# Moving the buffers that TensorE reads to whole kilobytes of a partition, in a two-layer decoder trunk

## The chip, the core and the metric

The kernel runs on one core of a Trainium2 chip. The metric is the device time of one execution in microseconds (us). It is given as the median of several runs. A separate execution is profiled, and its trace is what the views below come from. The engines are PE (TensorE, matmuls), PEld (TensorE's loads of stationary operands), DVE (VectorE), ACT (ScalarE), POOL (GpSimd) and SP (SyncE, which here issues the transfers).

## What is computed

The reference is a decoder of two layers on 256 tokens of width 2048, all in float32:

```python
h = x
for i in range(2):
    a = rmsnorm(h, attn_norm[i])
    h = h + (sb_dilated_mixer(a, ...) if i % 2 == 0 else fox_mixer(a, ...))   # q/k/v projection, 16 heads, output projection
    h = h + conv_ffn(rmsnorm(h, ffn_norm[i]), w_up[i], conv_w[i], conv_b[i], w_down[i])   # 2048 -> 2 x 5632 -> 2048
    gate = sigmoid(rmsnorm(h, ple_norm[i]) @ w_ple_gate[i])                    # 2048 -> 2048
    h = h + gate * (p[i] @ w_ple[i])                                           # 256 -> 2048
return rmsnorm(h, final_norm)
```

Layer 0's mixer has eight stick-breaking heads and eight heads of a dilated window. Layer 1's has 16 heads with forget gates. Nearly all of the arithmetic lies in the products with weights: `w_in` (2048 x 6144), `w_out`, `w_up` (2048 x 11264), `w_down` (5632 x 2048) and `w_ple_gate`.

## The kernel before

**Layout.** Activations lie with features on the 128 partitions and the 256 tokens along the free dimension. `h` holds 16 such slices. A product needs more precision than one pass of the one-pass type float32r gives, so both operands are split into a high and a low part (both float32r). `act0` and `act1` (line 114) hold an activation as `[128, 16, 2, 256]`: for each slice k of 128 features the 256 high parts and then the 256 low parts, which is 2 KB of a partition for each k. `pact` holds the same for the per-layer embedding.

**Weights.** They stream in once, in an order that the host prepares (`UNITS`, `GROUPS`). `issue_group` (line 144) loads up to 8 KB a partition into one of three `wr` buffers. `split_unit` (line 158) makes a unit's high part by a copy on ACT (line 165) and its low part by a subtraction on DVE (line 166), in one of four `w` buffers of 8 KB, as `[128, k, 2, 256]`. Up to three units stand ready ahead of TensorE (`LOOK`, line 170).

**Products.** `gemm_unit` (line 194) is the core. A unit has usually four slices k and 256 output features, taken as two halves j of 128. For each half TensorE runs, for the k of the unit, a matmul with the high weights as stationary operand and the 512 columns of `act[:, k]` (high and low) as moving stream (line 208), and then, for the same k, a matmul with the low weights and the 256 high columns `act[:, k, 0, :]` (line 211). So a half is a group of four streams of 512 columns and four of 256; in the down projection some units have three k. `gemm_v` (line 236) does the same for the value projection with the operands exchanged: the `w` buffer is streamed (lines 243 and 246) and 128 columns of `act` are loaded as weights. Where `flat` is set (line 199), and in the last product of all (line 736), there are three streams of 256 columns instead: high with high, high with low, low with high. `ple_up` (line 367) uses this with `pact`. `gemm_vf` (line 250) streams 272 columns of a `w` buffer.

**Around the products.** Each product goes to one of two PSUM buffers (`mm`). ACT copies one part out into a work tile `jn` or `jh`, DVE adds the other (lines 263 to 274). Work tiles of 2 KB come from the tag `t2` (line 134), which has seven buffers: `jn`, `jh`, `sq`, the two results `yg` and `yv` of a convolution group, `nd` and others. A buffer is given out again when its last reader is done. The attention is put among the units by a counter (`defer`, `tick`).

**Placement.** Pools get their place in the order in which they are opened, and tiles in a pool in the order in which they are made. Four small constants come first, so that the first pool, `cpool`, begins at byte 16,512 of a partition, 128 past a whole KB. By the addresses in the compiled kernel `h` lies there, `act0` at 32,896, `act1` at 65,664 and `pact` at 98,432 (all 128 past a whole KB), the three `wr` buffers at 138,432 and on and the four `w` buffers at 163,008, 171,200, 179,392 and 187,584 (all 192 past a whole KB). [...] Of the tiles that TensorE streams, one lies at a whole KB, the small `c2` of the forget gates (64 partitions, lines 491 and 493).

Of the kernel before, what the change touches and what calls it, by code (L numbers as in the profile page):

```python
# [10 lines left out]
F32 = mybir.dt.float32  # L11
F32R = mybir.dt.float32r
# [5 lines left out]
P = 128  # L18
D = 2048
S = 256  # L20
# [5 lines left out]
KT = D // P  # L26
# [78 lines left out]
def trunk(ctx: ExitStack, tc: tile.TileContext, xT, pT, pos, gains, conv, bf, cst, wst, out):  # L105
    nc = tc.nc

    cpool = ctx.enter_context(tc.tile_pool(name="cpool", bufs=1))
    wpool = ctx.enter_context(tc.tile_pool(name="wpool", bufs=1))
    work = ctx.enter_context(tc.tile_pool(name="work", bufs=1))  # L110
    psum = ctx.enter_context(tc.tile_pool(name="psum", bufs=1, space=bass.MemoryType.PSUM))

    h = cpool.tile([P, KT, S], F32, name="h")
    bufs = [cpool.tile([P, KT, 2, S], F32R, name=f"act{i}") for i in range(2)]
    pact = cpool.tile([P, 2, 2, S], F32R, name="pact")
    pl = cpool.tile([P, KT, S], F32, name="pl")
    gn = cpool.tile([P, 7, KT], F32, name="gn")
    cv = cpool.tile([P, DEPTH, 2 * FT, 4], F32, name="cv")
# [13 lines left out]
        return psum.tile([P, 2, 512], F32, name=name, tag="at", bufs=2)  # L132

    def t2_tile(name, shape=(P, 2, S), dt=F32):
        return work.tile(list(shape), dt, name=name, tag="t2", bufs=7)

    def t3_tile(name, shape=(P, 768), dt=F32):
        return work.tile(list(shape), dt, name=name, tag="t3", bufs=4)
# [124 lines left out]
    def joined(ps):  # L263
        t = t2_tile("jn")
        nc.scalar.copy(out=t, in_=ps[:, :, 1, :])  # L265
        nc.vector.tensor_add(out=t, in0=t, in1=ps[:, :, 0, :])  # L266
        return t

    def add_to_h(op, ps):
        hs = h[:, 2 * op:2 * op + 2, :]  # L270
        t = t2_tile("jh")
        nc.scalar.copy(out=t, in_=ps[:, :, 1, :])
        nc.vector.tensor_add(out=hs, in0=hs, in1=ps[:, :, 0, :])
        nc.vector.tensor_add(out=hs, in0=hs, in1=t)
# [17 lines left out]
    def norm_squares(op):  # L292
        hs = h[:, 2 * op:2 * op + 2, :]
        if op == 0:
            nc.scalar.activation(out=acc, in_=hs, func=AF.Square)
        else:
            sq = t2_tile("sq")
            nc.scalar.activation(out=sq, in_=hs, func=AF.Square)
            nc.vector.tensor_add(out=acc, in0=acc, in1=sq)
# [538 lines left out]
```

## Time and profile before

| | |
|---|---|
| median of 3 runs | 2476.81 us (2476.19 to 2476.83) |
| the profiled execution | 2476.15 us |
| its span, first to last instruction | 2474.4 us |
| granted TensorE clock, mean | 0.997 |
| busy: PE, PEld, DVE, ACT | 2453.4, 2145.1, 1715.1, 1320.2 us |
| moved by DMA | 457.20 MB, mean 185 GB/s |

A busy PE is not a PE at its peak: the profile gives the start of each matmul, and models its end, so a matmul's duration overlaps with the next one's. What a matmul costs in a row of them is the distance from its start to the start of the next. The timeline merges neighbours of one line into a row, "x4" for four, and the start of the following row closes the stretch.

### The profile page before, as it was taken

Reading aid. Unit: us, or ns where it says so; the run is one execution under the profiler, and the core shown is the slowest. Engines: PE = TensorE matmul, PEld = TensorE weight load, DVE = VectorE, ACT = ScalarE, POOL = GpSimd, SP = SyncE. Lnnn points to the kernel's source line nnn. Section 1 sums busy time; section 2 is a strip of 40 time slices with the busy share of each in tenths; the row PEclk is TensorE's granted clock in tenths of the full one; section 3 lists DMA queues with packets and bytes.
Section 4 is the critical chain, followed back from the end, with each engine's and each line's share of the span. In section 5 each row is a group of like instructions: output and inputs, shape, how many; then the busy total and the mean of one; then the engine's idle time right before and its main releaser. Section 6 shows DMA issues by size and latency. Waiting matters only on the chain. (4 is left out here: it accounts for less than half of the span.)

```text
span 2474.4 us, 34810 instructions
## 1 busy us (share of the span) xinstructions
PE 2453.4 (99%) x14270; PEld 2145.1 (87%) x14270; DVE 1715.1 (69%) x2386; ACT 1320.2 (53%) x1747; POOL 2.5 (0%) x8
## 2 busy tenths in 40 slices
PE   8999999999999999999999999999999999999997
PEld 7888888888888888888888888888888888888887
DVE  7767667776577657777765555677765776677776
ACT  6554455555455545556554444555544554455564
POOL 0000000000000000000000000000000000000000
PEclk9999999999999999999999999999999999999998
DMA  7444455555555555555454444555555555555553
GB/s 264 170 171 170 170 188 187 190 188 198 188 190 187 183 195 187 199 177 204 175 176 166 167 162 165 188 192 188 194 188 187 189 188 190 195 192 183 185 194 119
DMA packets 66431, 457.20 MB, mean 185 GB/s; under 512 B 7408, under 2 KB 7424, under 8 KB 16608
## 3 DMA queue, kind: packets, MB, share of 16 engines
q1 hardware_dynamic: 66096, 454.53, 51.9%
q8 instruction: 111, 1.82, 0.3%
q0 software_dynamic: 176, 0.46, 0.1%
q14 instruction: 48, 0.39, 0.0%
HBM read 452.86 MB, written 2.10 MB: 184 GB/s over the span
## 5 line engine op out<-in xcount | busy, mean ns | idle before, releaser
L166 DVE TENSOR_TENSOR w<-wr,w 128x1024 fp32r<-128x1024 f32 (+2 forms) x882 | 1049.2, 1191 | 500.0 <-ACT w L165 497.8
L165 ACT CAST w<-wr 128x1024 fp32r<-128x1024 f32 (+2 forms) x882 | 904.6, 1026 | 676.7 <-PE psd L211 179.2
L208 PE MATMUL psu<-act,w 128*128 128x512 f32 x2816 | 767.9, 394 | 0.0
L208 PEld LDWEIGHTS psu<-act,w 128*128 128x128 f32 x2816 | 476.7, 188 | 59.9
L211 PEld LDWEIGHTS psu<-act,w 128*128 128x128 f32 x2816 | 428.2, 188 | 63.8
L211 PE MATMUL psu<-act,w 128*128 128x256 f32 x2816 | 437.3, 277 | 0.0
L208 PE MATMUL psd<-act,w 128*128 128x512 f32 x1408 | 388.8, 394 | 0.0
L208 PEld LDWEIGHTS psd<-act,w 128*128 128x128 f32 x1408 | 236.4, 188 | 26.7
L211 PEld LDWEIGHTS psd<-act,w 128*128 128x128 f32 x1408 | 219.1, 188 | 34.7
L211 PE MATMUL psd<-act,w 128*128 128x256 f32 x1408 | 224.6, 278 | 0.0
L208 PE MATMUL psq<-act,w 128*128 128x512 f32 x512 | 141.6, 398 | 0.0
L208 PE MATMUL psk<-act,w 128*128 128x512 f32 x512 | 140.9, 396 | 0.0
L208 PE MATMUL pso<-act,w 128*128 128x512 f32 x512 | 140.0, 395 | 0.0
L243 PE MATMUL psv<-w,act 128*128 128x512 f32 x480 | 131.9, 397 | 0.2 <-DVE jn L266 0.2
L208 PE MATMUL psg<-act,w 128*128 128x512 f32 x480 | 131.1, 395 | 0.0
L265 ACT COPY jn<-psu 128x512 f32<-128x512 f32 x88 | 51.6, 587 | 142.4 <-PE psu L211 142.4
L266 DVE TENSOR_TENSOR jn<-jn,psu 128x512 f32<-128x512 f32 x88 | 60.4, 687 | 88.4 <-ACT jn L265 88.1
L208 PEld LDWEIGHTS psq<-act,w 128*128 128x128 f32 x512 | 86.9, 188 | 11.5 <-issue 0.2
L208 PEld LDWEIGHTS psk<-act,w 128*128 128x128 f32 x512 | 86.8, 188 | 11.2
L208 PEld LDWEIGHTS pso<-act,w 128*128 128x128 f32 x512 | 86.7, 188 | 11.0
L243 PEld LDWEIGHTS psv<-w,act 128*128 128x128 f32 x480 | 81.7, 188 | 11.8 <-PE psk L211 0.4
L208 PEld LDWEIGHTS psg<-act,w 128*128 128x128 f32 x480 | 81.3, 188 | 10.2
(202 smaller groups left out, 2143.1 us busy)
## 6 DMA issues: line engine op xcount, KB each, us to landing
wr<-in_w SPq DMA_DIRECT2D x388, 1024.0 KB, 4.8
wr<-in_w SPq DMA_DIRECT2D x36, 768.0 KB, 4.3
wr<-in_w SPq DMA_DIRECT2D x8, 896.0 KB, 4.6
wr<-in_w SPq DMA_DIRECT2D x7, 512.0 KB, 5.9
h<-in_x SPq DMA_DIRECT2D x4, 512.0 KB, 7.1
out_dram<-h SPq DMA_DIRECT2D x8, 256.0 KB, 2.4
wr<-in_w SPq DMA_DIRECT2D x2, 816.0 KB, 4.5
ct<-in_c SPq DMA_DIRECT2D x1, 841.0 KB, 6.2
```

Source lines behind the costliest of these rows:

```text
L165: nc.scalar.copy(out=w[:, :, 0, :], in_=raw)
L166: nc.vector.tensor_sub(out=w[:, :, 1, :], in0=raw, in1=w[:, :, 0, :].bitcast(F32))
L208: nc.tensor.matmul(ps[:, j], lhsT=w[:, k, 0, js], rhs=act[:, k0 - koff + k], start=first and k == 0, stop=False, skip_group_check=True)
L211: nc.tensor.matmul(ps[:, j, 1, :], lhsT=w[:, k, 1, js], rhs=act[:, k0 - koff + k, 0, :], start=False, stop=last and k == kc - 1, skip_grou ...
L243: nc.tensor.matmul(ps[:, t], lhsT=act[:, 4 * i + k, 0, tsl], rhs=w[:, k], start=i == 0 and k == 0, stop=False, skip_group_check=True)
L265: nc.scalar.copy(out=t, in_=ps[:, :, 1, :])
L266: nc.vector.tensor_add(out=t, in0=t, in1=ps[:, :, 0, :])
```

## The change

Two pools are opened first, a new `apool` and then `wpool`. A tile `head` of 896 bytes, which nothing reads or writes, is made first in `apool`, and the two activation buffers and `pact` move from `cpool` to `apool` behind it. 16,512 and 896 are 17,408, which is 17 KB. The sizes of what follows are whole KB (32, 32, 4, three times 8 and four times 8), so `act0`, `act1`, `pact`, the `wr` and the `w` buffers each begin at a whole KB. `cpool`, with `h` and the rest, comes behind them, and then the work pool. To make room, the tag `t2` has six buffers in place of seven. No instruction of the computation is added, removed or put elsewhere in the program.

```diff
+    apool = ctx.enter_context(tc.tile_pool(name="apool", bufs=1))
+    wpool = ctx.enter_context(tc.tile_pool(name="wpool", bufs=1))
     cpool = ctx.enter_context(tc.tile_pool(name="cpool", bufs=1))
-    wpool = ctx.enter_context(tc.tile_pool(name="wpool", bufs=1))
     work = ctx.enter_context(tc.tile_pool(name="work", bufs=1))
...
+    apool.tile([P, 224], F32, name="head")
+    bufs = [apool.tile([P, KT, 2, S], F32R, name=f"act{i}") for i in range(2)]
+    pact = apool.tile([P, 2, 2, S], F32R, name="pact")
     h = cpool.tile([P, KT, S], F32, name="h")
-    bufs = [cpool.tile([P, KT, 2, S], F32R, name=f"act{i}") for i in range(2)]
-    pact = cpool.tile([P, 2, 2, S], F32R, name="pact")
...
     def t2_tile(name, shape=(P, 2, S), dt=F32):
-        return work.tile(list(shape), dt, name=name, tag="t2", bufs=7)
+        return work.tile(list(shape), dt, name=name, tag="t2", bufs=6)
```

## The prediction

> **What bounds the kernel now.** I read the page first, its busy times and its groups.
>
> ```profile
> span 2474.4 us, 34810 instructions
> PE 2453.4 (99%) x14270; PEld 2145.1 (87%) x14270; DVE 1715.1 (69%) x2386; ACT 1320.2 (53%) x1747; POOL 2.5 (0%) x8
> L208 PE MATMUL psu<-act,w 128*128 128x512 f32 x2816 | 767.9, 394 | 0.0
> L211 PE MATMUL psu<-act,w 128*128 128x256 f32 x2816 | 437.3, 277 | 0.0
> L208 PE MATMUL psd<-act,w 128*128 128x512 f32 x1408 | 388.8, 394 | 0.0
> L208 PE MATMUL psq<-act,w 128*128 128x512 f32 x512 | 141.6, 398 | 0.0
> L208 PE MATMUL psk<-act,w 128*128 128x512 f32 x512 | 140.9, 396 | 0.0
> L208 PE MATMUL pso<-act,w 128*128 128x512 f32 x512 | 140.0, 395 | 0.0
> L243 PE MATMUL psv<-w,act 128*128 128x512 f32 x480 | 131.9, 397 | 0.2 <-DVE jn L266 0.2
> L208 PE MATMUL psg<-act,w 128*128 128x512 f32 x480 | 131.1, 395 | 0.0
> ```
>
> The last column of the groups is idle time ahead of them: next to none on PE. The view of the waits, for PE alone, says the same of the whole kernel; its rows add up to 11.7 us, and the largest lie at the start (`psp`) and in the tail (`rps`, `nps`).
>
> ```profile
> PE psp L203 <- ACT w L165: 5.7, 2, 5.5
> PE rps L333 <- DVE nd L331: 2.7, 1, 2.7
> PE nps L308 <- DVE sq L747: 1.6, 1, 1.6
> ```
>
> So the kernel is as long as its streams, and only a change in the pace of a stream can move its time by much. The timeline of PE alone, inside the feed-forward part, gives that pace:
>
> ```profile
> 702.61 1.09 PE L208 MATMUL psu<-act,w 128*128 128x512 f32 x4
> 703.54 0.62 PE L211 MATMUL psu<-act,w 128*128 128x256 f32 x4
> 704.00 1.09 PE L208 MATMUL psu<-act,w 128*128 128x512 f32 x4
> ...
> 710.47 0.62 PE L211 MATMUL psu<-act,w 128*128 128x256 f32 x4
> 710.93 0.85 PE L208 MATMUL psu<-act,w 128*128 128x512 f32 x3
> ```
>
> From 702.61 to 710.93 there are six groups of four streams of 512 and four of 256 columns, 8.32 us, or 1.387 us a group. A group streams 4 x 2 + 4 x 1 = 12 KB of a partition, so one KB (256 float32 columns) takes 115.6 ns. The x-counts of the seven rows of 512 columns above add to 6,720, which is 1,680 groups; 1,680 x 1.387 us = 2,330 us, 94% of the span.
>
> 115.6 ns is a mean of two paces. The same timeline at the runs of 256 columns alone shows both:
>
> ```profile
> 1266.42 1.52 PE L203 MATMUL psp<-pact,w 128*128 128x256 f32 x12
> 1267.78 0.62 PE L208 MATMUL psq<-act,w 128*128 128x512 f32 x2
> ...
> 1308.21 1.58 PE L203 MATMUL psp<-pact,w 128*128 128x256 f32 x12
> 1309.62 1.10 PE L208 MATMUL psq<-act,w 128*128 128x512 f32 x4
> ...
> 2447.61 5.60 PE L736 MATMUL pse<-act,w 128*128 128x256 f32 x48
> 2453.05 5.61 PE L736 MATMUL psg<-act,w 128*128 128x256 f32 x48
> ```
>
> Twelve streams from `pact` take 1.36 us (113.3 ns each) the first time and 1.41 us (117.5 ns) the second; the 48 of the last product take 5.44 us, 113.3 ns each again. I call them the quick and the slow pace. 115.6 lies about half way.
>
> **The change part by part.** *The new places.* Streams from `act0`, `act1` and `pact` now begin 128 bytes past a whole KB, weights 192 past; afterwards both begin at a whole KB (weights of the second half j at 512 past one). The number of streams, their length and the stationary loads stay. So the sum has one term, 12 KB x 1,680 groups x the change in the pace of a KB: one nanosecond on a KB is 20.2 us. The trace has no streams of this kind at a whole KB (the small `c2` streams 64 partitions against a broadcast weight, and its neighbours' loads hide its pace), so I bound the pace by its neighbours: 113.3 ns, the quick one, is 2.2 ns less than now, -45 us; 117.5 ns, the slow one, is 1.9 ns more, +39 us. Neither can be excluded by a reason.
>
> Which of the rows is nearest? In the two `psp` runs above the stream is the same bytes of `pact`, and the weights lie in `w` buffers that differ by a multiple of 8 KB, so that the offset in a KB is the same too; yet the paces differ. There the offset does not decide, but the state in which a run is entered does. On the other side stand the value projections, where `w` is streamed (192 past a KB) and `act` is loaded (128 past):
>
> ```profile
> 1294.58 1.08 PE L243 MATMUL psv<-w,act 128*128 128x512 f32 x4
> 1295.49 0.63 PE L246 MATMUL psv<-w,act 128*128 128x256 f32 x4
> 1295.96 1.09 PE L243 MATMUL psv<-w,act 128*128 128x512 f32 x4
> 1296.89 0.62 PE L246 MATMUL psv<-w,act 128*128 128x256 f32 x4
> 1297.35 1.07 PE L243 MATMUL psv<-w,act 128*128 128x512 f32 x4
> ```
>
> The shapes are those of `psu`, but the groups alternate: 0.91 and 0.47 us, then 0.93 and 0.46, where `psu` has 0.93 and 0.46 each time. So the offsets (or the buffers) do change the order of quick and slow. But two groups take 2.77 us, 1.385 each, against 1.387: other offsets, the same mean. This is the nearest row to an edit that moves both operands and keeps the shapes, and I take its answer: the pace stays at about 115.5 ns, and the term is -0.1 ns x 20.2 = -2 us, within what can be told from nothing.
>
> [...]
>
> *Six buffers of `t2` for seven.* No wait on PE appears as long as the PSUM buffers are emptied in time. In the feed-forward part a group uses four of these tiles (`yg`, `yv`, two `jn`), so with six the seventh, the first `jn` of the next group, gets the buffer of `yg`, whose last reader is line 279:
>
> ```profile
> 570.59 0.69 DVE L279 TENSOR_TENSOR act<-yg,act 128x512 fp32r<-128x512 f32 x1
> ...
> 573.85 0.59 ACT L265 COPY jn<-psu 128x512 f32<-128x512 f32 x1 [1.68 <-PE psu L211]
> ```
>
> These two rows are from the timelines of DVE and ACT. The reader ends at 571.28, the next writer starts at 573.85 after its product, so 2.57 us lie between and the cost is nothing. If that cover were gone, ACT's copy would wait, and behind it in ACT's queue the copies of weight units (line 165), of which two to three stand ready ahead of PE. Where `yg`, `yv`, `nd` and its two parts live at once, after a norm, one buffer is left for `jn`; that is at four places, and a microsecond at each would be 4 us at most. I take nothing.
>
> *The rest moves too.* `h`, `ct` and the small tiles get other addresses, and transfers into `wr` begin at a whole KB. These serve DVE, ACT and DMA, of which the first is busy for 69% of the span; the tail after the last product (2458.5 to 2474.4, 16 us) would have to change by a third before it showed.
>
> Sum: profiled 2476.15 us, -2 at most, nothing else. The median of the runs is 0.66 us above the profiled execution, so I forecast the median itself, 2476.0 us, with a range of its own from 2471.9 to 2481.8 (plus and minus 0.2%, about what a measurement of this kernel can tell from no change).
>
> **The rivals.** *The quick pace for all.* With weights and stream at the same offset, the groups stay in the state of line 736 and of the quick `psp` run: 12 x 113.3 = 1.360 us a group, 1,680 x 27 ns = 45 us less, 2431 us. For it: the change takes the difference of 64 bytes between the two operands to zero, and the value projection shows that offsets reorder the paces. Against it: the quick runs are themselves at the old offsets.
>
> *A border between KBs costs.* A stream of 256 columns that starts 128 past a KB crosses one border, one of 512 crosses two; at whole KBs it is none and one. The price from rows: streams of full float32, the scores of a stick-breaking head, move their columns at a slower pace, and do not show it:
>
> ```profile
> 51.42 1.02 PE L445 MATMUL scs<-q,k 128*128 128x256 f32 x4
> 52.28 0.61 PE L448 MATMUL scs<-q,k 128*128 128x128 f32 x4
> ```
>
> 0.86 us for four is 215 ns. If that is two cycles a column, one cycle a column would be 107.5 ns a KB, and the quick 113.3 would hold 5.8 ns for one border (an estimate). A group loses eight borders, 46 ns, and the kernel 78 us: 2399 us. Against it: nothing in the trace separates a border from a cost that every KB has wherever it starts. [...]
>
> *The slow pace for all.* This one ends on the other side. If the stationary load, which runs beside the stream, and the stream hold each other up where they touch the same part of the memory at the same time, then starting both at a whole KB is the worst place, and the slow `psp` run is what every KB gets: 12 x 117.5 = 1.410 us, 1,680 x 23 ns = 39 us more, 2516 us. It decides where more than 6 in 10 of the KBs go slow (6 of 12 would be 12 x 115.4, as now). For it: slow runs exist in which twelve streams in a row are all slow. Against it: at the old offsets the state comes and goes.
>
> *The change does not do what it says.* `head` has no reader; if it gets no room, the buffers stay 128 past a KB, and the time is that of the forecast.
>
> **How the numbers follow.** No change of the pace, or no change of the places: 0.40 (0.03 of it the last rival). The quick pace, in whole or in good part: 0.24. Borders: 0.12. The slow pace, in whole or in part: 0.24. So faster by over 0.2% has 0.36, within 0.2% 0.40, slower 0.24. The forecast's own range leaves out 6 in 10, so the range must reach to both paces: from 2425, a little below the quick one, to 2518, just past the slow one. Left out are the borders and a little beyond the slow pace, some 0.16.
>
> **What would show it.** Right, if the timeline has groups of 1.385 to 1.389 us in `psu` and `psd`, whatever the order of 0.93 and 0.46 in them, and PE has no new waits. The quick rival shows 0.91 and 0.45 in every group; the slow one 0.94 and 0.47; borders show 256-column streams under 113 ns, in line 736 first, where nothing else runs. If `head` got no room, every row would agree with before to the digit. A wait of PE on ACT at `jn` or `jh` would show that the seventh buffer was needed. The forecast is wrong if the mean of a KB leaves 115.4 to 115.8 ns.

## The result, and the profile after

The change makes the kernel slower: 2500.82 us median of 3 runs (2500.07 to 2501.03) against 2476.81 us, a ratio of 1.0097 with a 95% interval from 1.0074 to 1.012. The forecast was no change, 2476.0 us. That is outside the forecast's own 2471.9 to 2481.8; it lies inside the wide range (2425 to 2518), on the side that had 0.24.

The page of the changed kernel, its span, busy times and the two largest groups of matmuls (three more lines stand above the code now, so line 208 is 211, 211 is 214 and 736 is 739):

```profile
span 2499.2 us, 34809 instructions
PE 2479.4 (99%) x14270; PEld 2170.6 (87%) x14270; DVE 1715.6 (69%) x2386; ACT 1317.7 (53%) x1747; POOL 2.5 (0%) x8
L211 PE MATMUL psu<-act,w 128*128 128x512 f32 x2816 | 768.9, 394 | 0.0
L214 PE MATMUL psu<-act,w 128*128 128x256 f32 x2816 | 448.2, 281 | 0.0
```

The span is 24.8 us longer and PE is busy for 26.0 us more with the same 14,270 matmuls. DVE and ACT are as before, and so is the granted clock of TensorE (0.997). The streams of 512 columns keep their mean of 394 ns; those of 256 went from 277 to 281. (These durations have a modelled end; their difference is what can be read.) PE's waits, in the view of waits, are the old ones:

```profile
PE psp L206 <- ACT w L168: 5.4, 1, 5.4
PE rps L336 <- DVE nd L334: 2.7, 1, 2.7
PE nps L311 <- DVE sq L750: 1.6, 1, 1.6
PE psp L206 <- ACT pl L374: 1.3, 1, 1.3
```

The value projection waits 0.2 us for DVE at a `jn`, as it did before; PE has no other wait at `jn` or `jh`, and none on ACT there, so the seventh `t2` buffer was not missed. The timeline of PE in the feed-forward part, and at the last product:

```profile
703.04 1.09 PE L211 MATMUL psu<-act,w 128*128 128x512 f32 x4
703.97 0.64 PE L214 MATMUL psu<-act,w 128*128 128x256 f32 x4
704.45 1.09 PE L211 MATMUL psu<-act,w 128*128 128x512 f32 x4
705.38 0.63 PE L214 MATMUL psu<-act,w 128*128 128x256 f32 x4
...
711.46 0.86 PE L211 MATMUL psu<-act,w 128*128 128x512 f32 x3
...
2471.83 5.92 PE L739 MATMUL pse<-act,w 128*128 128x256 f32 x48
2477.59 5.92 PE L739 MATMUL psg<-act,w 128*128 128x256 f32 x48
```

Six groups from 703.04 to 711.46 take 8.42 us, 1.403 us each for 1.387 before. Four streams of 512 columns still take 0.93 us, four of 256 now 0.47 to 0.48 for 0.46 before. In the last product 48 streams take 5.76 us, 120.0 ns each for 113.3 before. Taken over the starts of all `psu` streams, one of 512 columns takes 232.3 ns (232.2 before) and one of 256 takes 118.5 (114.6 before). From start to start, all streams of 256 columns together take 25.0 us more than before, which is the whole of the loss.

The last product also says where to look. While its second row runs (from 2477.59 to 2483.35) no weights are prepared any more: the last split of a unit (line 169) ends at 2475.20, and the DMA moves nothing (a share of 0.00, 0 GB/s from 2477.6 to 2483.3). ACT and DVE still work on other tiles (`h`, `acc`, `gt`, `sq`), but TensorE alone reads `act` and `w`. Its two readers are the moving stream and the load of the next stationary operand: 48 of each, 5.92 us busy and 5.83.

### The profile page after: what moved, and what is told of

The parts are those of the page before. It is cut to its first block, busy times and chain, and to the rows that moved or that the text cites. A ratio compares the mean times of both kernels' runs of the same rounds, so it can differ in the third digit from the quotient of the medians.

```text
span 2499.2 us, 34809 instructions
## 1 busy us (share of the span) xinstructions
PE 2479.4 (99%) x14270; PEld 2170.6 (87%) x14270; DVE 1715.6 (69%) x2386; ACT 1317.7 (53%) x1747; POOL 2.5 (0%) x8
## 5 line engine op out<-in xcount | busy, mean ns | idle before, releaser
L214 PE MATMUL psu<-act,w 128*128 128x256 f32 x2816 | 448.2, 281 | 0.0
L246 PEld LDWEIGHTS psv<-w,act 128*128 128x128 f32 x480 | 82.3, 188 | 11.9 <-PE psk L214 0.4
```

Of the source, the lines that this page charges most:

```text
L214: nc.tensor.matmul(ps[:, j, 1, :], lhsT=w[:, k, 1, js], rhs=act[:, k0 - koff + k, 0, :], start=False, stop=last and k == kc - 1, skip_grou ...
L246: nc.tensor.matmul(ps[:, t], lhsT=act[:, 4 * i + k, 0, tsl], rhs=w[:, k], start=i == 0 and k == 0, stop=False, skip_group_check=True)
```

## The experiments

The common question is which property of the new places counts. I write *distance* for the start of the weight buffers less the start of the streamed buffers, within a KB: 64 bytes before, 0 after. Each kernel below is the changed kernel with other padding (`head` ahead of `act0`, a new `pad` ahead of the `wr` and `w` buffers), unless its text says more. The granted clock is 0.997 or 0.998 in all of their profiled executions, so the clock explains none of the differences.

**The old offsets at the new places.**

```diff
-    apool.tile([P, 224], F32, name="head")
+    wpool.tile([P, 16], F32, name="pad")
```

> The changed kernel with its old offsets: the streamed buffers begin 128 bytes past a whole KB and the weight buffers 192 past, as before, while the order of the pools, the places of h and of the small tiles, and the six t2 buffers stay as changed. Theory A (what counts is the distance between where the stream and where the stationary operand begin: 64 before, 0 after): 2477 us, streams of 256 columns back at 113.3 to 115 ns, 113.3 in the last product. Theory B (what counts is that the stream itself begins at a whole KB): 2477 us as well. Theory C (what counts is that the stationary operand begins at one): 2477 us. Theory D (the slow-down comes from the moved pools or from the seventh t2 buffer): 2501 us.

Measured: 2476.47 us, ratio 0.9995 (0.9986 to 1.0005). Theory D is out: neither the order of the pools nor the six buffers cost anything. `h` and the small tiles shift along with `pad` (`h` begins 192 bytes past a whole KB here, and at a whole KB after the change), so they are not quite where the change put them; the next two kernels, one with the loss and one without, have `h` 128 and 64 past.

**Distance 0 away from a whole KB.** Neither `head` nor `pad`.

> Streamed buffers and weight buffers both begin 128 past a whole KB: distance 0, but nothing at a whole KB. Theory A (distance): 2501 us, 118.5 ns for a stream of 256 columns and 120 in the last product. Theories B and C (whole KB of the stream, of the stationary operand): 2477 us. Theory D (pools, t2): 2501 us.

Measured: 2502.14 us, ratio 1.0098 (1.0082 to 1.0113). No buffer begins at a whole KB, and the whole loss is there. The last product, in the timeline of PE:

```profile
2473.43 5.92 PE L739 MATMUL pse<-act,w 128*128 128x256 f32 x48
2479.18 5.92 PE L739 MATMUL psg<-act,w 128*128 128x256 f32 x48
```

5.75 us for 48 is 119.8 ns.

**Distance 64 with the streams at a whole KB.** `head` as in the change, `pad` of 64 bytes.

> Streamed buffers at a whole KB, weight buffers 64 past one: the distance of before, with the stream at a whole KB. Theory A (distance): 2477 us. Theory B (stream at a whole KB): 2501 us. Theory C (stationary operand at a whole KB): 2477 us. Theory D (pools, t2): 2501 us.

Measured: 2476.27 us, ratio 0.9996 (0.9987 to 1.0006). The same two rows of the timeline:

```profile
2448.03 5.60 PE L739 MATMUL pse<-act,w 128*128 128x256 f32 x48
2453.47 5.61 PE L739 MATMUL psg<-act,w 128*128 128x256 f32 x48
```

5.44 us, 113.3 ns, as before. With these two, theories B and C fall: a stream at a whole KB neither gained nor cost (2476.27 us), the loss came without weights at a whole KB (2502.14 us), and what is left is the distance, 0 there and 64 here.

**Distance -128, weights at a whole KB.** No `head`, `pad` of 896 bytes.

> Streamed buffers 128 past a whole KB as before, weight buffers at a whole KB: a distance of -128 (384 in steps of the 512 bytes between the two halves of a weight unit). Theory A (distance): neither the 64 of before nor the 0 of after, so a time of its own, somewhere from 2431 (all streams quick) to 2516 us. Theory B (stream at a whole KB): 2477 us. Theory C (stationary operand at a whole KB): 2501 us. Theory D (pools, t2): 2501 us.

Measured: 2503.01 us, ratio 1.0102 (1.0085 to 1.0119). This kernel alone would have spoken for theory C; beside the second experiment, where no weights lie at a whole KB, it is one more bad distance. Its pace is its own: 118.7 ns a stream in the last product, not 119.8.

**A scan of distances.** Streams 128 past a KB, `pad` of 32, 128 and 192 bytes, and later 96.

> Streamed buffers 128 past a whole KB, weight buffers 160 past: a distance of 32 bytes. So far distance 64 gave 2476 us at two places, 0 gave 2501 and 2502, and -128 gave 2503. Theory A1 (only a distance that is an odd multiple of 64 bytes is good): about 2501 us, 118 ns for a stream of 256 columns. Theory A2 (the start of the stationary load must be some tens of bytes ahead of the stream, and the more the better): between 2477 and 2501. Theory A3 (0 and -128 are bad because they are multiples of 128, everything else is good): 2477 us.

Measured: 2503.43 us, ratio 1.0106 (1.0091 to 1.0121). Theory A3 had 2477 us here and falls, and theory A2's range ends at 2501.

> Streamed buffers 128 past a whole KB, weight buffers 256 past: a distance of +128. Theory A1 (odd multiples of 64 good): about 2502 us. Theory A2 (the stationary operand ahead of the stream is good, behind or level with it is bad): 2477 us or less. Theory A3 (multiples of 128 bad): about 2502 us.

Measured: 2501.82 us, ratio 1.01 (1.0085 to 1.0116). The last product has the same two rows, to the digit of the duration, as at distance -128 (first here, then there):

```profile
2472.00 5.86 PE L739 MATMUL pse<-act,w 128*128 128x256 f32 x48
2477.70 5.86 PE L739 MATMUL psg<-act,w 128*128 128x256 f32 x48
```

```profile
2473.92 5.86 PE L739 MATMUL pse<-act,w 128*128 128x256 f32 x48
2479.62 5.86 PE L739 MATMUL psg<-act,w 128*128 128x256 f32 x48
```

With it theory A2 falls. +128 and -128 differ by 256, so a period of 256 bytes would make the two kernels alike. These rows alone do not show it, since the kernel at a distance of 96 further down has them too:

```profile
2488.06 5.86 PE L739 MATMUL pse<-act,w 128*128 128x256 f32 x48
2493.76 5.86 PE L739 MATMUL psg<-act,w 128*128 128x256 f32 x48
```

The value projections speak for it: by place in the group, their eight streams take the same times at +128 and at -128, to within 0.3 ns. The groups of `psu` do not (119.6 ns at one and 121.6 at the other for the second stream of 256 columns), so the match is not complete.

> Streamed buffers 128 past a whole KB, weight buffers 320 past: a distance of +192, an odd multiple of 64. Theories A1 and A3: 2477 us, streams of 256 columns at 114.6 ns in psu. Theory A2 (ahead is good): 2477 us or less. If the distance counts only within 512 bytes in some finer way, a time of its own between 2431 and 2516.

Measured: 2472.82 us, ratio 0.9984 (0.9974 to 0.9993). Of the three theories only A1 is left, which has odd multiples of 64 as the good places. In the timeline of `psu` the groups now alternate as the value projection's did before:

```profile
702.96 1.09 PE L211 MATMUL psu<-act,w 128*128 128x512 f32 x4
703.89 0.62 PE L214 MATMUL psu<-act,w 128*128 128x256 f32 x4
704.34 1.07 PE L211 MATMUL psu<-act,w 128*128 128x512 f32 x4
705.25 0.63 PE L214 MATMUL psu<-act,w 128*128 128x256 f32 x4
705.73 0.63 PE L211 MATMUL psu<-act,w 128*128 128x512 f32 x2
```

0.93 and 0.45, then 0.91 and 0.48. There the operands are exchanged, so the distance was -64, and -64 and 192 differ by 256, as a period of 256 bytes would have it. Over all groups the match is close. The eight places of the value projection before take 229.8, 232.3, 230.5, 228.5, 115.6, 116.0, 115.5 and 116.0 ns, those of `psu` here 229.8, 232.6, 230.4, 228.4, 115.7, 115.9, 115.5 and 115.0.

> Streamed buffers 128 past a whole KB, weight buffers 224 past: a distance of 96 bytes. So far, distances 64 and 192 are good (2476 and 2473 us), 0, 32 and 128 bad (2501 to 2503). If only odd multiples of 64 are good: about 2502 us. If the good places are broad, around 64 and beyond it: about 2476 us.

Measured: 2515.84 us, ratio 1.0157 (1.0139 to 1.0176), the worst of all. Here the streams of 512 columns take part: 233.7 ns in `psu`, over all starts, and 118.9 for 256. The good place at 64 is not broad: 64 gave 2476.5 and 2476.3 us, 32 gave 2503.4, and 96 gave 2515.8. Theory A1 has the sign right, but its 2502 us is 14 us short.

**The distance of 192 at the place of the change.** `head` of 896 bytes as in the change, `pad` of 192.

> The changed kernel with its streamed buffers left at a whole KB and its weight buffers moved 192 bytes past one: the distance that gave 2472.8 us, at the place of the change. If the distance alone counts: 2472.8 us, 0.15% faster than before and 1.1% faster than the change, and the same order of paces (234, 236, 229, 231 for four streams of 512 columns, then all of 256 at 113.5 or all at 118). If 2472.8 was an accident of the other places: 2476 us.

Measured: 2470.77 us, ratio 0.9975 (0.9965 to 0.9985). So the version that was to be tried, with its streams at a whole KB, is faster than before by 0.25% once its weights are put 192 bytes on. Where it gains, from its page:

```profile
L211 PE MATMUL psu<-act,w 128*128 128x512 f32 x2816 | 763.0, 393 | 0.0
L214 PE MATMUL psu<-act,w 128*128 128x256 f32 x2816 | 439.4, 278 | 0.0
```

Over all starts of `psu` it is 230.4 ns for 512 columns (232.2 before) and 115.5 for 256 (114.6 before): 0.9 ns less a pair, 2.4 us over the 2,816 of them. The down projection (`psd`) gains another 3.0 us. It does not keep the quick pace; the last product runs at 117.8 ns.

The down projection is also where this kernel and the other one at 192 (2472.82 us) part, though their distance is the same. The first row is of that one's groups, the second of this one's:

```profile
L214 PE MATMUL psd<-act,w 128*128 128x256 f32 x1408 | 226.2, 279 | 0.0
```

```profile
L214 PE MATMUL psd<-act,w 128*128 128x256 f32 x1408 | 224.1, 277 | 0.0
```

In the 128 groups with three k, the streams of 256 columns take 117.4 to 119.9 ns there and 113.2 to 113.5 here, and such a group takes 1,053 and 1,027 ns (1,043 before). That is 3.4 us. So the distance did not fix everything; why the two kernels fall into different paces there stays open.

**All streams of 256 columns, at the old distance.** The core of the edit; both drains now take only one part of the PSUM tile (`add_to_h` likewise):

```diff
-    def gemm(ps, act, kind, l, c0, cuts, k0=0, koff=0, part=None, flat=False):
+    def gemm(ps, act, kind, l, c0, cuts, k0=0, koff=0, part=None, flat=True):
...
-        nc.scalar.copy(out=t, in_=ps[:, :, 1, :])
-        nc.vector.tensor_add(out=t, in0=t, in1=ps[:, :, 0, :])
+        nc.scalar.copy(out=t, in_=ps[:, :, 0, :])
```

> Old offsets (distance 64), but three streams of 256 columns for each k in every product that had one of 512 and one of 256, except the value projections; the drain then copies or adds one part of a PSUM tile in place of two. Columns streamed stay the same; stationary loads rise by half. 1,560 groups are changed. If such streams keep the quick pace of the last product (113.3 ns a KB for 115.6): 1,560 x 27 ns = 42 us less, 2435 us. If they fall into the slow pace (117.5): 36 us more, 2513 us. If the pace stays a mixture of both by the state in which each unit is entered, as in the per-layer embedding's products: about 2477 us.

Measured: 2498.78 us, ratio 1.0087 (1.0072 to 1.0102). From its page and, behind it, from the timeline of its last product:

```profile
L206 PE MATMUL psu<-act,w 128*128 128x256 f32 x8448 | 995.8, 281 | 0.0
...
2469.30 5.82 PE L739 MATMUL pse<-act,w 128*128 128x256 f32 x48
2474.95 5.82 PE L739 MATMUL psg<-act,w 128*128 128x256 f32 x48
```

The last product runs at 117.7 ns although its code, operands and distance are those of before, where it ran at 113.3. Only what ran ahead of it differs. At distance 64 both paces lasted over long rows, as this kernel's timeline shows:

```profile
328.62 73.70 PE L206 MATMUL pso<-act,w 128*128 128x256 f32 x648
402.15 1.07 PE L206 MATMUL psu<-act,w 128*128 128x256 f32 x8
...
416.64 166.94 PE L206 MATMUL psu<-act,w 128*128 128x256 f32 x1416
583.41 0.87 PE L206 MATMUL psd<-act,w 128*128 128x256 f32 x6
```

648 streams in a row take 113.5 ns each, and 1,416 take 117.8. Apart from waits of PE and the first few streams after a break, the pace of a row in this kernel changes only at breaks where other streams come between, such as those of a norm or of the attention. In the kernel before, the mixture of 512 and 256 columns seems to set the pace anew in every group of `psu`: in the mean over all groups the first of the four streams of 256 takes 118.4 ns, the other three 113.3. What it is at a break that sets the pace isn't shown.

**Two distances within one weight buffer.** Two kernels with streams at a whole KB and only one of the two parts of the weights moved by 64 bytes. The buffers are 8,448 bytes (33 x 256), so the four of them begin 0, 256, 512 and 768 past a whole KB, and the distances named here hold within 256 bytes. The first has `HI, LO = 0, 1`, the second 1, 0:

```diff
-        w = w[:, :2 * kc * cw].rearrange("p (k s c) -> p k s c", s=2, c=cw)
-        nc.scalar.copy(out=w[:, :, 0, :], in_=raw)
+        w = w[:, :2080].rearrange("p (s x) -> p s x", s=2)[:, :, :kc * cw].rearrange("p s (k c) -> p k s c", c=cw)
+        nc.scalar.copy(out=w[:, :, HI, :], in_=raw)
```

> The changed kernel (streams at a whole KB, high weights at distance 0), with the low weights moved 64 bytes on inside each weight buffer (the buffers grow to 8,448 bytes). The stationary load for the next matmul runs beside the stream of the present one, so beside three of four streams of 256 columns runs a load of low weights (now at 64), and beside the fourth and three of the four of 512 columns one of high weights (at 0). Theory E (the load that runs beside a stream holds it up, by its distance): in psu three of four streams of 256 columns come back to some 114.6 ns and the fourth stays at 118 to 120, 12 ns a group of 1,560, about 2482 us. Theory F (one distance for the whole group, set by its first operand): stays at 2501 us. Theory G (a stream is held up by its own weights): all four of 256 columns come back, 1,560 x 16 ns, 2476 us.

Measured: 2496.02 us, ratio 1.0077 (1.0063 to 1.0091). The four streams of 256 columns take 118.3, 117.5, 117.4 and 120.0 ns by their place in the group, over all `psu` starts.

> The counterpart: high weights 64 bytes on from the stream, low weights at distance 0. Theory E (the load beside): only one of four streams of 256 columns has a load at distance 64 beside it, so 118 ns or more for three and some 114 for one, 4 ns a group, about 2495 us; the streams of 512 columns keep their mean of 232 ns. Theory F (the group's first operand): back to 2476 us. Theory G (a stream's own weights): stays at 2501 us.

Measured: 2489.44 us, ratio 1.0051 (1.0035 to 1.0066). The four places take 115.8, 112.5, 116.7 and 116.7 ns. The first row is of the first kernel's page, the second of this one's:

```profile
L214 PE MATMUL psu<-act,w 128*128 128x256 f32 x2816 | 447.9, 281 | 0.0
```

```profile
L214 PE MATMUL psu<-act,w 128*128 128x256 f32 x2816 | 438.6, 277 | 0.0
```

No theory holds. E wanted three of four streams near 114.6 in the first kernel and has none. G wanted all four there. F has the sign right, since the place of the high weights moves the streams of 256 columns most, but not the times: 2489 where 2476 was expected, 2496 where 2501 was. In both kernels the value projection streams two pieces that lie apart. That this costs something isn't shown: 512 columns take 236 to 237 ns there, and 234 to 237 in the other kernels. What sets the pace at each place of a group stays open.

## Why the prediction was wrong, point by point

**What bounds the kernel: right.** It is as long as its streams. The whole difference is in their pace, and PE has no new wait. (Two slips change nothing: the waits add up to 11.9 us, not 11.7, and 2 us off the median would be 2474.8 us, not 2476.0.)

**The term, 12 KB x 1,680 groups x the change of a KB's pace: right in form.** A KB went from 115.56 to 116.94 ns (8.32 and 8.42 us through 72), 1.38 x 20.2 = 28 us by that one stretch, for 24.8 in the span.

**The value taken for it: wrong, and this is the step that failed.** The prediction took the value projection as "the nearest row to an edit that moves both operands and keeps the shapes" and read from it "other offsets, the same mean". The offsets there were not other in the sense that counts. They were the mirror image, a distance of -64 for +64, two of the good places. The change goes to 0, for which the prediction had no row. Two rows at good places were read as a proof that all places are equal. The pace of a KB was to stay at about 115.5 ns, and came out at 116.9. The row does answer for a change to 192: over all its groups it has 115.35 ns a KB, and the kernels at 192 have 115.28 in `psu`.

**The two `psp` runs: read half right.** "There the offset does not decide, but the state in which a run is entered does" is what the kernel of equal streams shows (113.5 or 117.8 ns at the same distance). But that holds at distance 64, and was used against any effect of the distance. At distance 0 the last product ran at 120.0 and 119.8 ns in the two kernels that have it, slower than either.

**The rivals.** The slow pace for all had the right sign, and it named what counts: both operands starting at the same offset is a bad place (2500.8 and 2502.1 us), though not the worst one, since 96 is worse (2515.8) and 32 and 128 are as bad (2503.4 and 2501.8). That the two hold each other up in the memory, its reason, was not shown. Its size was off. It put every KB at 117.5 ns, +39 us; measured, the streams of 256 columns went to 118.5, while those of 512 stayed at 232.3, or 116.2 a KB, so some 25 us. Its sign, 0.94 and 0.47 us in a group, came for the second part alone (0.93 and 0.47 to 0.48). The quick pace for all asked for the distance to be taken to zero, which is what brought the loss. Borders between KBs fall with the distance of 64 at a whole KB: the streams cross one border less each there, and the time is 2476.3 us. The 5.8 ns for a border came from the author's estimate that the 215 ns of a float32 stream are two cycles a column, which no run shows. That `head` gets no room is out: in the compiled kernel `act0` begins at 17,408. The prediction also had the wrong time for this rival. Without `head` the new order of the pools alone would have put the weights 128 past a whole KB, the same as the streams; that is the second experiment, 2502.14 us and not the forecast's.

**The covers that were costed at nothing held.** Six `t2` buffers and moved small tiles are in the first experiment, at 0.9995 of the time before.

## What to carry to other kernels

In this kernel, where TensorE streams float32r back to back and loads a new stationary operand for every stream, the distance between the two operands' start addresses was worth 1% to 2% of the time: 64 and 192 bytes were good (2471 to 2477 us), 0, 32, 96 and 128 bad (2501 to 2516), and 1.8% lay between the best kernel and the worst (2470.77 and 2515.84 us). It is cheap to try (a pad of some bytes ahead of one pool), and a tile of 64 bytes ahead of the weights took it from 0 to 64 here (2502.14 to 2476.47 us), so compare the start addresses before a small difference is put down to something else. And one row at another place that has the same time does not show that place is indifferent; ask whether the two places differ in what could matter.

## What the runs showed of the hardware that was not expected

- The pace of a stream of 256 float32r columns changed with the distance of its operands: 113.3 or 117.7 ns at 64 bytes (by what ran ahead), 117.8 at 192, 119.8 to 120.0 at 0, 118.7 at 128, -128 and 96, 118.3 at 32, in the last product.
- The distance seems to count within 256 bytes: 192 in `psu` has the order of paces that -64 had in `psv`, to within 1.0 ns at each of the eight places. The place past a whole KB counted for little beside it: distance 64 gave 2476.5 and 2476.3 us at two places, distance 0 gave 2500.8 and 2502.1, and 192 gave 2472.8 and 2470.8.
- In the kernel of equal streams, at a distance of 64, a long row kept one of two paces (113.5 ns over 648 streams, 117.8 over 1,416), and the pace changed at breaks where other streams came between.
- In the last product of the changed kernel TensorE alone reads `act` and `w`, and the pace there went from 113.3 to 120.0 ns. Why the distance changes it was not shown: the two kernels that moved one part of the weights by 64 bytes took 2496.02 and 2489.44 us, which no theory had for both.
